# Weight low parts on one engine, modulation work spread anew: a two-layer hybrid backbone on one core

## The chip, the core and the metric

The kernel runs on one core of a Trainium2 chip. Its time is the device time of one execution in microseconds, the median of the runs shown. The engines are named as in the profile: TensorE (PE, its weight loads PEld), VectorE (DVE), ScalarE (ACT), GpSimd (POOL) and SyncE (SP), whose queue issues the weights' transfers.

## The reference

256 latent tokens and 256 context tokens of 1024 channels pass two layers. A layer is a SwiGLU half-step, four parallel token mixers with a gated merge, and a second half-step; each of the three has a norm that is shifted and scaled by vectors (modulation), which come from the conditioning vectors `c` and `c_ctx` by a large matrix product. Cut to what matters:

```python
def adaln(cvec, w, b):
    m = jax.nn.silu(cvec) @ w + b            # nine vectors of 1024 per layer
...
def ffn_half_step(s, g, mods, j, w1, w3, w2):
    h = modulate(rmsnorm(s, g), mods[j], mods[j + 1])
    return s + 0.5 * mods[j + 2] * swiglu(h, w1, w3, w2)
...
for i in range(DEPTH):
    x = ffn_half_step(x, ..., m_lat, 0, ...);  ctx = ffn_half_step(ctx, ..., m_ctx, 0, ...)
    # mixers: bidirectional gated linear attention (a scan), spatial gating, 2-D DFT, short convolution
    y = merge(h, branches, w_branch[i], w_gate[i], b_gate[i], w_out[i])
    x = x + m_lat[5] * y
    x = ffn_half_step(x, ..., m_lat, 6, ...)
    # the context gets the same in layer 0; in layer 1 it is only read by the scan
return rmsnorm(x, g_final)
```

The mixers are added up as `sigmoid(h @ w_gate[k] + b_gate[k]) * (branch[k] @ w_branch[k])` over the four branches, and the sum goes through `w_out`.

## The kernel before

Activations lie with channels on the partitions and the 512 tokens (latent 0 to 255, context 256 to 511) along the free axis. Every weight tile (128x1024) is used in a split form: `hi` is the tile cast to float32r by ScalarE (L79), `lo` is what the cast lost, `raw - hi` (L82); every activation has `hh` and `hl` in the same way. A product is three passes of matmuls (`passes`, L321): hi x hh, hi x hl, lo x hh.

The six stages are called here FFN 1 (layer 0, first half-step), mixer 1, FFN 2, FFN 3 (layer 1, first half-step), mixer 2 and FFN 4. FFN 4 and most of mixer 2 have the latent tokens alone, 256 columns; the others have both, 512.

The program is a list of units that `_Program` walks through in order; a unit has weight tiles and a function that issues the matmuls. Two rings of four buffers hold raw and split tiles. When a unit has used a tile it calls `release`, and `ahead` splits the next one, so four tiles are split in advance, in program order. Each engine has one queue and takes its instructions in that order. A tile whose entry has the mark "pool" gets its low part on GpSimd, others on VectorE. The marks come from tables (`DPOOL`, `HPOOL`, `DPOOL1`, `TPOOL`, `CPOOL`): every second up tile (w3), most w2 tiles where both streams run, two or four tiles of a head, some tiles of the merge and the convolution. `hold_lows` keeps low parts back from the end of a stage's tail until the next head calls `flush`.

A half-step has three parts (`PARTS`: 8, 8 and 6 tiles of the hidden axis). Each part has up steps (w1 and w3, `glu` makes the instructions g, L547, cast and gl, L335) and eight down steps (w2). In the third part the last three w2 tiles are the tail (`tail_group`): latent columns first, then context; after each product come the residual on VectorE (`residual`, L531), a square on ScalarE and its sum on GpSimd (`add_sq`, L366). The next stage's norm begins in the tail: `Norm.ms` sums the squares over channels by a matmul (L393), takes the power on GpSimd, `diag` (L402) makes a diagonal `dg` of it, `bc` (L406) spreads it by a matmul, and `scaled`, `high` and `low` make hn, hh and hl. `head_group` is the first unit of a stage; it starts with four tiles on the latent half (`pair_hi`, L450, where both streams run).

The modulation vectors are computed on VectorE by 128 modulation units (`ada_unit`, L290), each a 128x1024 tile of the modulation matrix with one instruction per conditioning vector (multiply, and sum along the free axis). 96 units have two (`junk` and `ada_raw`), the last 32 have one. `PHASES` says how many units `weave` puts behind a step of each kind, and `phase_end` how many must be through at the end of a stage: 32, 48, 80, 112, 120, 128.

In a mixer the scan (`gla_stream`) runs as a side program: after every so many columns of matmuls `tick` lets it go on to its next `yield`. Its seven levels end in score matmuls (lv, L709). Then come products K and Q (L717 to L721), transposes kt (L739), updates u (L748), and two blocks of outputs o (L781), each followed by square, sum, power and scaling into W (L784 to L789). `proj_r` drains what is left of the scan and, 24 matmuls later, transposes W (oT, L1118).

Of the kernel before, what the change touches and what calls it, by code (L numbers as in the profile page):

```python
# [7 lines left out]
F32 = mybir.dt.float32  # L8
# [36 lines left out]
class _Program:  # L45
# [28 lines left out]

    def split(self, raw, n, eng=None):
        nc, pool = self.nc, self.pool
        hi = pool.tile([128, 1024], F32R, tag="whi", name="whi", bufs=RING)
        lo = pool.tile([128, 1024], F32R, tag="wlo", name="wlo", bufs=RING)
        nc.scalar.copy(hi[:, :n], raw[:, :n])  # L79

        def low():
            (eng or nc.vector).tensor_tensor(lo[:, :n], raw[:, :n], hi[:, :n].bitcast(F32), ALU.subtract)  # L82

        if self.hold_lows:
            self.lows.append(low)
        else:
            low()
        return hi, lo
# [43 lines left out]
    def ahead(self, need=-1):  # L132
        while True:
            self.fetch_ahead(need)
            if self.ns >= len(self.todo):
                return
            f = self.todo[self.ns]
            uj, spec = self.flat[f]
            if self.raws[f] is None or self.held >= (self.limit if uj > need else RING):
                return  # L140
            self.held += 1
            self.fetched["w"] -= 1
            t = self.split(*self.raws[f], eng=self.nc.gpsimd if len(spec) > 2 else None)
            self.got.setdefault(uj, []).append(t)
            self.ns += 1
# [31 lines left out]
def kernel(ctx: ExitStack, tc: tile.TileContext, I, out: bass.AP):  # L177
# [203 lines left out]
    class Norm:  # L381
# [17 lines left out]
        def diag(self):  # L399
            ms = self.r  # L400
            dg = self.dg = tmp("dg")[:, 0:256].rearrange("p (u i) -> p u i", u=2)
            V.tensor_tensor(dg, ident.unsqueeze(1).to_broadcast([128, 2, 128]),  # L402
                            ms[:, 2:4].unsqueeze(2).to_broadcast([128, 2, 128]), ALU.mult)

# [27 lines left out]
        def low(self, c):  # L432
            l, m, st = self.l, self.m, c[0] // 256
            a, b = c[0], c[0] + c[1]
            for d in range(KT):
                t, hh = self.t[c][d], st8["hh"][:, d, a:b].bitcast(F32)
                if d % 2:
                    S.activation(out=t, in_=t, func=AF.Identity, bias=mod(l, m, d, st), scale=1.0)
                    G.tensor_tensor(st8["hl"][:, d, a:b], t, hh, ALU.subtract)  # L439
                else:  # L440
                    V.scalar_tensor_tensor(st8["hl"][:, d, a:b], t, mod(l, m, d, st), hh, ALU.add, ALU.subtract)

# [11 lines left out]
    def head_group(ws, accs, streams, done, skip=()):  # L454
# [42 lines left out]
    def tail_group(ds_, ws, rhs, nk, streams, gate, after, nxt):  # L497
# [21 lines left out]
        if CTX not in streams:  # L519
# [15 lines left out]
    def add_ffn(l, s, m, streams, after, weave, nxt):  # L535
# [63 lines left out]
        for pi, (f0, nf) in enumerate(PARTS):  # L599
            fs = list(range(f0, f0 + nf))  # L600
            if pi == 0:
                hw = [w(n, f) for f in (0, 1) for n in ("w1", "w3")]
                hw = [h + ("pool",) * (i in HPOOL[0 if l + s == 0 else len(streams)]) for i, h in enumerate(hw)]
                P.add(hw, head)
# [4 lines left out]
            for f in fs:  # L609
                P.add([w("w1", f), w("w3", f) + ("pool",)], up(f))  # L610
                if l == 0 and s == 0 and f == 2:
# [6 lines left out]
            def w2c(d):  # L618
                pl = ("pool",) if (d >= DPOOL if len(streams) == 2 else d in DPOOL1) else ()
                return ("w", I["w2"][l, s, d][:, f0 * 128:(f0 + nf) * 128]) + pl  # L620

# [12 lines left out]
    def gla_stream(l, c, A, want_o):  # L634
# [84 lines left out]
        if want_o:  # L719
            V.tensor_tensor(Q[lo_], Wr[lo_, :, tok], X[lo_], ALU.mult)  # L720
            V.tensor_tensor(Q[hi_], Wl[hi_, :, tok], Y[hi_], ALU.mult)  # L721
        yield

# [75 lines left out]
    def add_mixer(l, both, after, weave, nxt):  # L799
# [38 lines left out]

        P.add([wT(h) + ("pool",) * (h in HPOOL[2]) for h in range(4)], head)

# [255 lines left out]
        def add_terms(k, first=False, last=False, each=lambda dp: None):  # L1096
            for dp in range(4):
                pl = [("pool",) if i in TPOOL[l][k] else () for i in range(3)]
                P.add([("w", I["wgate"][l, k, 2 * dp]) + pl[0], ("w", I["wgate"][l, k, 2 * dp + 1]) + pl[1],
                       ("w", I["wbranch"][l, k, dp]) + pl[2]], term(k, dp, first, last))  # L1100
                each(dp)

        add_terms(1, first=True)
        for t_ in range(4):
            ws = [wT(i + t_) + (("pool",) if n in CPOOL[l] else ()) for n, i in enumerate((20, 24, 16))]
            P.add(ws, proj_conv(t_))
        add_terms(2)
# [25 lines left out]
        for h in range(4):  # L1133
            P.add([wT(4 + h)], proj_r(h))
            if h == 0:
                P.add([], load_cond)
# [48 lines left out]
    PHASES = [  # L1185
        (32, dict(head=0, up0=0.5, up=0.2, down0=1.25, down1=1.5, down2=1.2)),
        (48, dict(r=1, term0=3, term1=4, term2=3, term3=0, wout=1)),
        (80, dict(head=0, up0=0.5, up=0.2, down0=1.25, down1=1.5, down2=1.2)),
        (112, dict(head=0, up0=0.5, up=0.2, down0=1.25, down1=1.5, down2=1.2)),
        (120, dict(r=1, term0=1.5, term1=1.5, term2=1.5, term3=1.5, wout=0)),  # L1190
        (128, dict(head=2, up0=1, up=0, down0=0, down1=0, down2=0)),
    ]
# [177 lines left out]
```

## Time and profile before

| | |
|---|---|
| median of 3 runs | 2275.84 us (2275.73 to 2279.39) |
| profiled execution, its own time | 2279.79 us |
| span of the profiled execution | 2277.8 us |
| TensorE busy | 2214.9 us |
| VectorE busy | 1364.2 us, 1857 instructions |
| ScalarE busy | 769.9 us |
| GpSimd busy | 743.9 us, 437 instructions |
| transfers | 330.43 MB, 145 GB/s over the span |

Busy times overlap. Time in a stage is lost where TensorE stops, and the stages stop for different reasons, so the shares of the whole span say little: one has to find the stops in TensorE's timeline, and look at what the engine that is waited for was doing just before. The granted clock of TensorE is 1.00 (2.4 GHz) in most windows of 20 us and lower in those that contain a stop and the restart behind it.

### The profile page before, as it was taken

To read this page: it belongs to the slowest core of one execution; us is meant where nothing else is said; L and a number is where in the kernel's file an instruction comes from. 1 tells how busy PE (TensorE), PEld (TensorE's weight loads), DVE (VectorE), ACT (ScalarE), POOL (GpSimd) and SP (SyncE) were. 2 spreads that over 40 slices of the span, in tenths; PEclk is the share of its full clock that TensorE was granted. 3 is DMA by queue.
4 is the path that set the end of the run, shared out by engine and by line. 5 is a ranking of instruction groups with operands and counts; after the bars stand their busy time and mean duration, and the time that the engine had idled before them with its cause. 6 is when DMAs were issued, how large, how long until landed. Compare 5 with 4: busy or idle time off the path is not lost.

```text
span 2277.8 us, 31627 instructions
## 1 busy us (share of the span) xinstructions
PE 2214.9 (97%) x12718; PEld 1950.2 (86%) x12718; DVE 1364.2 (60%) x1857; ACT 769.9 (34%) x1090; POOL 743.9 (33%) x437
## 2 busy tenths in 40 slices
PE   6999999899999999999999999999999998998998
PEld 4888888898888888798888888888889998998998
DVE  4474575566657736853837464654435788875644
ACT  3322222443232223243232233222234553345443
POOL 1232425322213314142323263323334245424222
PEclk9999999999999999999999999999999999999999
DMA  7454454422222234523535433443544453485663
GB/s 271 158 164 150 132 180 140 128 82 69 89 84 84 84 111 153 208 99 123 176 129 167 137 112 122 154 151 120 185 148 146 137 166 106 142 278 191 223 187 115
DMA packets 98563, 330.43 MB, mean 145 GB/s; under 512 B 11505, under 2 KB 17649, under 8 KB 98161
## 3 DMA queue, kind: packets, MB, share of 16 engines
q1 hardware_dynamic: 90480, 315.91, 42.5%
q10 hardware_dynamic: 7936, 12.50, 1.5%
q8 instruction: 100, 1.64, 0.3%
q14 instruction: 47, 0.38, 0.0%
HBM read 322.08 MB, written 6.29 MB: 144 GB/s over the span
## 4 chain that ended last, share of the span: by engine, by line
PE 84%; DVE 8%; issue 2%; DMA 2%; ACT 2%; POOL 2%; POOLq 0%; DVEq 0%; ACTq 0%; SPq 0%
PE mm L321 74%; PE mm L867 4%; PE dn L321 1%; DVE ada_raw L290 1%; PE lv L709 1%; DVE junk L290 1%; DVE wlo L82 1%; DMA ada_raw<-in_wadaT_dram 1%; ACT whi L79 1%; POOL wlo L82 1%; DMA x<-in_xT_dram 1%; ACT hh L429 1%; DMA raw<-in_w_dram 1%; PE mm L450 1%; PE ms L393 0%
## 5 line engine op out<-in xcount | busy, mean ns | idle before, releaser
L321 PE MATMUL mm<-hh,whi 128*128 128x512 f32 (+1 forms) x2448 | 843.8, 349 | 3.3 <-ACT hh L429 2.3
L321 PE MATMUL mm<-hh,wlo 128*128 128x512 f32 (+1 forms) x2448 | 837.8, 346 | 6.3 <-DVE wlo L82 4.1
L321 PE MATMUL mm<-hl,whi 128*128 128x512 f32 (+1 forms) x2512 | 808.9, 343 | 0.1
L82 POOL TENSOR_TENSOR wlo<-raw,whi 128x1024 fp32r<-128x1024 f32 (+1 forms) x183 | 472.0, 2582 | 900.7 <-ACT whi L79 872.6
L79 ACT CAST whi<-raw 128x1024 fp32r<-128x1024 f32 (+2 forms) x458 | 469.0, 1032 | 751.5 <-PE mm L321 412.9
L82 DVE TENSOR_TENSOR wlo<-raw,whi 128x1024 fp32r<-128x1024 f32 (+3 forms) x275 | 349.4, 1276 | 352.9 <-ACT whi L79 349.4
L321 PEld LDWEIGHTS mm<-hh,wlo 128*128 128x128 f32 x2448 | 468.5, 191 | 62.8 <-DVE wlo L82 5.1
L321 PEld LDWEIGHTS mm<-hh,whi 128*128 128x128 f32 x2448 | 469.0, 192 | 59.3 <-ACT hh L429 3.2
L321 PEld LDWEIGHTS mm<-hl,whi 128*128 128x128 f32 x2512 | 454.2, 190 | 54.3 <-POOL hl L439 0.3
L290 DVE SCALAR_TENSOR_TENSOR ada_raw<-ada_raw,condb 128x1024 f32<-128x1024 f32 x128 | 250.1, 1956 | 18.0 <-DMA ada_raw<-in_wadaT_dram 14.7
L321 PE MATMUL mm<-gh,whi 128*128 128x512 f32 (+1 forms) x710 | 248.6, 350 | 0.0
L321 PE MATMUL mm<-gl,whi 128*128 128x512 f32 (+1 forms) x710 | 247.7, 349 | 0.0
L321 PE MATMUL mm<-gh,wlo 128*128 128x512 f32 (+1 forms) x710 | 247.5, 349 | 0.0
L547 DVE TENSOR_TENSOR g<-sg,mm 128x512 f32<-128x512 f32 (+1 forms) x88 | 54.5, 620 | 247.5 <-PE mm L321 243.0
L334 ACT CAST gh<-g 128x512 fp32r<-128x512 f32 (+1 forms) x88 | 49.9, 567 | 352.0 <-DVE g L547 352.0
L290 DVE SCALAR_TENSOR_TENSOR junk<-ada_raw,condb 128x1024 f32<-128x1024 f32 x96 | 147.3, 1535 | 10.5 <-DMA ada_raw<-in_wadaT_dram 10.3
L321 PEld LDWEIGHTS mm<-gh,whi 128*128 128x128 f32 x710 | 136.1, 192 | 16.9
L321 PEld LDWEIGHTS mm<-gl,whi 128*128 128x128 f32 x710 | 136.0, 192 | 16.9
L321 PEld LDWEIGHTS mm<-gh,wlo 128*128 128x128 f32 x710 | 136.0, 191 | 16.5
L531 DVE SCALAR_TENSOR_TENSOR x<-mm,mods,x 128x256 f32<-128x256 f32 x180 | 78.5, 476 | 28.7 <-PE mm L321 28.5
L335 DVE TENSOR_TENSOR gl<-g,gh 128x512 fp32r<-128x512 f32 (+1 forms) x88 | 58.8, 668 | 55.7 <-ACT gh L334 55.7
L366 POOL TENSOR_TENSOR sq<-sq,sqt 128x256 f32<-128x256 f32 (+1 forms) x44 | 50.2, 1140 | 104.5 <-ACT sqt L365 103.5
(222 smaller groups left out, 2360.3 us busy)
## 6 DMA issues: line engine op xcount, KB each, us to landing
raw<-in_w_dram SPq DMA_DIRECT2D x240, 512.0 KB, 3.6
ada_raw<-in_wadaT_dram SPq DMA_DIRECT2D x128, 512.0 KB, 4.4
raw<-in_wgate_dram SPq DMA_DIRECT2D x64, 512.0 KB, 3.7
raw<-in_winT_dram SPq DMA_DIRECT2D x56, 512.0 KB, 3.4
raw<-in_wbranch_dram SPq DMA_DIRECT2D x32, 512.0 KB, 3.6
raw<-in_w_dram SPq DMA_DIRECT2D x32, 384.0 KB, 3.1
ada_raw<-in_wada_dram SPq DMA_DIRECT2D x16, 512.0 KB, 6.2
raw<-in_wout_dram SPq DMA_DIRECT2D x16, 512.0 KB, 5.8
```

Of the source, the lines that this page charges most:

```text
L79: nc.scalar.copy(hi[:, :n], raw[:, :n])
L82: (eng or nc.vector).tensor_tensor(lo[:, :n], raw[:, :n], hi[:, :n].bitcast(F32), ALU.subtract)
L290: V.scalar_tensor_tensor(o, raw, 1.0, ada["c"][st], ALU.mult, ALU.mult, accum_out=mods[l][:, 8 * m + d, st:st + 1])
L321: T.matmul(acc[:, c0:c0 + cw], lhsT=a, rhs=b[:, c0:c0 + cw], start=bool(first and i == 0), stop=bool(last and i == n - 1))
L334: S.copy(dst_hi[:, a:b], src[:, a:b])
L335: V.tensor_tensor(dst_lo[:, a:b], src[:, a:b], dst_hi[:, a:b].bitcast(F32), ALU.subtract)
L366: eng.tensor_tensor(sq[:, a:b], sq[:, a:b], t[:, a:b], ALU.add)
L429: S.activation(out=st8["hh"][:, d, a:b], in_=self.t[c][d], func=AF.Identity, bias=mod(l, m, d, st), scale=1.0)
L450: T.matmul(acc[:, sl], lhsT=w3(w[part])[:, k, :], rhs=hsrc(k)[0][:, sl], start=(k == 0 and part == 0), stop=False)
L531: V.scalar_tensor_tensor(x[:, d, a:b], acc[:, a:b], gate(d, s[0] // 256), x[:, d, a:b], ALU.mult, ALU.add)
L547: V.tensor_tensor(g[:, a:b], sg[:, a:b], p3[:, a:b], ALU.mult)
L867: T.matmul(p[:, 0:width], lhsT=x_, rhs=w_[:, u, :], start=(k + i == 0), stop=(k == KT - 1 and i == 2))
```

## The change

All low parts of weight tiles go to VectorE, and the tables that marked tiles for GpSimd are gone. The odd halves of `hl`, which ScalarE and GpSimd made, are made on VectorE like the even ones. `diag` has two instructions with a scalar operand in place of one with two tensors. Low parts are also held from the single-stream tail (end of mixer 2) to the head of FFN 4. In the scan one `yield` becomes `yield 2`: the piece behind it, the transposes kt, comes two ticks later instead of one. The modulation units are all done by the end of FFN 3, by 40, 48, 88 and 128 at the end of the first four stages, with none in the third part's down steps and none in mixer 2 and FFN 4; so the conditioning vectors are not loaded again in mixer 2.

```diff
-DPOOL = 1
-HPOOL = ((), (0, 1, 2, 3), (0, 1))
...
-DPOOL1 = ()
-TPOOL = (((0, 1, 2), (), (), ()), ((0,), (0,), (0,), ()))
-CPOOL = ((), (0,))
...
         def low():
-            (eng or nc.vector).tensor_tensor(lo[:, :n], raw[:, :n], hi[:, :n].bitcast(F32), ALU.subtract)
+            nc.vector.tensor_tensor(lo[:, :n], raw[:, :n], hi[:, :n].bitcast(F32), ALU.subtract)
...
-            V.tensor_tensor(dg, ident.unsqueeze(1).to_broadcast([128, 2, 128]),
-                            ms[:, 2:4].unsqueeze(2).to_broadcast([128, 2, 128]), ALU.mult)
+            for u in range(2):
+                V.tensor_scalar(dg[:, u, :], ident, ms[:, 2 + u:3 + u], None, ALU.mult)
...
-                if d % 2:
-                    S.activation(out=t, in_=t, func=AF.Identity, bias=mod(l, m, d, st), scale=1.0)
-                    G.tensor_tensor(st8["hl"][:, d, a:b], t, hh, ALU.subtract)
-                else:
-                    V.scalar_tensor_tensor(st8["hl"][:, d, a:b], t, mod(l, m, d, st), hh, ALU.add, ALU.subtract)
+                V.scalar_tensor_tensor(st8["hl"][:, d, a:b], t, mod(l, m, d, st), hh, ALU.add, ALU.subtract)
...
                 if CTX not in streams:
+                    P.hold_lows = False
+                    P.flush()
                     N.low(LAT)
...
             N.diag()
             for _ in ds_:
                 P.release()
+                P.hold_lows = True
...
-                P.add([w("w1", f), w("w3", f) + ("pool",)], up(f))
+                P.add([w("w1", f), w("w3", f)], up(f))
...
             V.tensor_tensor(Q[hi_], Wl[hi_, :, tok], Y[hi_], ALU.mult)
-        yield
+        yield 2
...
-            if h == 0:
+            if h == 0 and both:
                 P.add([], load_cond)
...
     PHASES = [
-        (32, dict(head=0, up0=0.5, up=0.2, down0=1.25, down1=1.5, down2=1.2)),
-        (48, dict(r=1, term0=3, term1=4, term2=3, term3=0, wout=1)),
-        (80, dict(head=0, up0=0.5, up=0.2, down0=1.25, down1=1.5, down2=1.2)),
-        (112, dict(head=0, up0=0.5, up=0.2, down0=1.25, down1=1.5, down2=1.2)),
-        (120, dict(r=1, term0=1.5, term1=1.5, term2=1.5, term3=1.5, wout=0)),
-        (128, dict(head=2, up0=1, up=0, down0=0, down1=0, down2=0)),
+        (40, dict(head=0, up0=1, up=1.15, down0=1, down1=1.25, down2=0)),
+        (48, dict(r=1, term0=3, term1=3, term2=0, term3=0, wout=0)),
+        (88, dict(head=0, up0=0.8, up=1.15, down0=1, down1=1.5, down2=0)),
+        (128, dict(head=0, up0=0.8, up=1.15, down0=1, down1=1.5, down2=0)),
     ]
```

Every other place where a tile had the mark "pool" loses it in the same way. In the orders below the changed kernel has its own line numbers (L77 is the low part, L285 the modulation unit, L525 the residual).

VectorE at the end of FFN 1, in part 3's down steps, before (x is the residual, mods the sum that ends a group of eight units):

```order
L290 SCALAR_TENSOR_TENSOR junk,mods_87<-ada_raw,condb 128x1024
L290 SCALAR_TENSOR_TENSOR ada_raw,mods_87<-ada_raw,condb 128x1024
L531 SCALAR_TENSOR_TENSOR x<-mm,mods_87,x 128x256 x4
...
L531 SCALAR_TENSOR_TENSOR x<-mm,mods_87,x 128x256 x2
...
L294 TENSOR_TENSOR mods_87<-mods_87,bada 128x16
L531 SCALAR_TENSOR_TENSOR x<-mm,mods_87,x 128x256 x5
L396 TENSOR_SCALAR ms<-ms 128x2
```

The same place in the change:

```order
L77 TENSOR_TENSOR wlo<-raw,whi 128x768 x2
L525 SCALAR_TENSOR_TENSOR x<-mm,mods_87,x 128x256 x4
L77 TENSOR_TENSOR wlo<-raw,whi 128x768
L525 SCALAR_TENSOR_TENSOR x<-mm,mods_87,x 128x256 x2
L77 TENSOR_TENSOR wlo<-raw,whi 128x768
L525 SCALAR_TENSOR_TENSOR x<-mm,mods_87,x 128x256 x2
L77 TENSOR_TENSOR wlo<-raw,whi 128x1024
L525 SCALAR_TENSOR_TENSOR x<-mm,mods_87,x 128x256 x5
L391 TENSOR_SCALAR ms<-ms 128x2
```

Between two steps' residuals stood a unit of two instructions; there is now one low part.

VectorE at the end of the scan in mixer 2, from the scaling of the first block of outputs to the first `proj_r` (W is the scaled output, sig a term of the merge, rs the product that takes the transposed W), before:

```order
L789 TENSOR_TENSOR W<-o,oms 128x4x128
L82 TENSOR_TENSOR wlo<-raw,whi 128x1024
L1080 TENSOR_TENSOR sig<-sig,mm 128x256
L82 TENSOR_TENSOR wlo<-raw,whi 128x1024
L786 TENSOR_REDUCE oms<-Y 128x4
L787 TENSOR_SCALAR oms<-oms 128x4
L789 TENSOR_TENSOR W<-o,oms 128x4x128
L82 TENSOR_TENSOR wlo<-raw,whi 128x1024
L1080 TENSOR_TENSOR sig<-sig,mm 128x256
...
L1121 SCALAR_TENSOR_TENSOR rs<-mm,ggla,rs 128x256
```

The same place in the change:

```order
L781 TENSOR_TENSOR W<-o,oms 128x4x128
L77 TENSOR_TENSOR wlo<-raw,whi 128x1024
L1072 TENSOR_TENSOR sig<-sig,mm 128x256
L778 TENSOR_REDUCE oms<-Y 128x4
L779 TENSOR_SCALAR oms<-oms 128x4
L781 TENSOR_TENSOR W<-o,oms 128x4x128
L77 TENSOR_TENSOR wlo<-raw,whi 128x1024
L1111 SCALAR_TENSOR_TENSOR rs<-mm,ggla,rs 128x256
```

The second block's sum came after one more tile, and the last two terms of the merge behind it; it now comes right behind the first block's, and `proj_r` right behind that. On TensorE 36 matmuls stood between the two blocks of outputs and 60 between the second and oT; now none and 24.

## Rows read from the trace of the kernel before

**Rows 1.** The page's first part: busy time of each engine.
```profile
PE 2214.9 (97%) x12718; PEld 1950.2 (86%) x12718; DVE 1364.2 (60%) x1857; ACT 769.9 (34%) x1090; POOL 743.9 (33%) x437
```
**Rows 2.** Chain that ended last, mixer 1: start us, us, what.
```profile
734.02 12.26 PE mm L321 x54
```
**Rows 3.** Timeline of FFN 1: start us, us, engine, line, operation, out<-in, idle before.
```profile
88.01 0.69 DVE L335 TENSOR_TENSOR gl<-g,gh 128x512 fp32r<-128x512 f32 x1 [0.69 <-ACT gh L334]
88.61 1.22 DVE L290 SCALAR_TENSOR_TENSOR junk<-ada_raw,condb 128x1024 f32<-128x1024 f32 x1
89.01 3.08 POOL L82 TENSOR_TENSOR wlo<-raw,whi 128x1024 fp32r<-128x1024 f32 x1 [8.49 <-ACT whi L79]
...
89.88 3.29 DVE L290 SCALAR_TENSOR_TENSOR ada_raw<-ada_raw,condb 128x1024 f32<-128x1024 f32 x1
```
**Rows 4.** Groups by form: busy us, mean ns | idle before.
```profile
L82 POOL TENSOR_TENSOR wlo<-raw,whi 128x1024 fp32r<-128x1024 f32 x162 | 425.0, 2625 | 849.1 <-ACT whi L79 821.1 <-issue 13.8 <-DMA bgate<-in_bgate_dram 7.7
L82 DVE TENSOR_TENSOR wlo<-raw,whi 128x1024 fp32r<-128x1024 f32 x258 | 332.2, 1293 | 323.0 <-ACT whi L79 319.5 <-PE sgu L946 2.3 <-PE mm L321 0.5
...
L290 DVE SCALAR_TENSOR_TENSOR ada_raw<-ada_raw,condb 128x1024 f32<-128x1024 f32 x128 | 250.1, 1956 | 18.0 <-DMA ada_raw<-in_wadaT_dram 14.7
...
L290 DVE SCALAR_TENSOR_TENSOR junk<-ada_raw,condb 128x1024 f32<-128x1024 f32 x96 | 147.3, 1535 | 10.5 <-DMA ada_raw<-in_wadaT_dram 10.3
```
**Rows 5.** Groups by form: the residual.
```profile
L531 DVE SCALAR_TENSOR_TENSOR x<-mm,mods,x 128x256 f32<-128x256 f32 x180 | 78.5, 476 | 28.7 <-PE mm L321 28.5
```
**Rows 6.** Timeline of TensorE, tails of FFN 1, 2 and 3.
```profile
389.64 0.28 PE L321 MATMUL mm<-gh,whi 128*128 128x256 f32 x1
...
403.44 1.87 PE L393 MATMUL ms<-ones,sq 128*128 128x1 f32 x8 [5.00 <-POOL sq L366]
...
411.42 0.40 PE L450 MATMUL mm<-hh,whi 128*128 128x256 f32 x2
...
1338.89 0.28 PE L321 MATMUL mm<-gh,whi 128*128 128x256 f32 x1
...
1359.62 0.40 PE L450 MATMUL mm<-hh,whi 128*128 128x256 f32 x2
...
1709.91 0.28 PE L321 MATMUL mm<-gh,whi 128*128 128x256 f32 x1
...
1724.17 0.40 PE L450 MATMUL mm<-hh,whi 128*128 128x256 f32 x2
```
**Rows 7.** Windows, end of mixer 1: PE, PEld, DVE, ACT, POOL busy, PEclk, DMA share, GB/s.
```profile
940.00:960.00 20.00, 16.34 (x63) 12.42 (x62) 15.50 (x22) 6.60 (x8) 1.54 (x1) 0.91 0.68 263
```
**Rows 8.** Windows from one block of score matmuls to the next, mixer 2.
```profile
1886.69:1901.69 15.00, 12.26 (x90) 12.06 (x90) 13.42 (x15) 4.49 (x7) 8.29 (x5) 0.89 0.39 128
1901.69:1914.83 13.14, 11.28 (x91) 10.56 (x89) 11.84 (x15) 5.28 (x8) 6.03 (x4) 1.00 0.39 127
1914.83:1927.30 12.47, 10.90 (x88) 10.52 (x89) 9.80 (x12) 3.87 (x6) 8.48 (x6) 1.00 0.40 129
...
1939.70:1950.54 10.84, 10.66 (x88) 10.48 (x89) 10.51 (x13) 3.90 (x5) 7.04 (x5) 1.00 0.48 147
```
**Rows 9.** Timeline of TensorE, the two blocks of transposes kt in mixer 2.
```profile
1841.85 1.06 PE L739 MATMUL kt<-ident,K 128*128 128x128 f32 x8 [1.38 <-DVE K L718]
...
1971.21 1.49 PE L739 MATMUL kt<-ident,K 128*128 128x128 f32 x8 [3.51 <-DVE K L718]
```
**Rows 10.** Timeline of TensorE and VectorE: the second block of outputs in mixer 2.
```profile
1991.72 0.39 PE L782 MATMUL o<-S,Q 128*128 128x128 f32 x2
...
1994.80 0.69 DVE L789 TENSOR_TENSOR W<-o,oms 128x512 f32<-128x512 f32 x1 [1.13 <-POOL oms L788]
```
**Rows 11.** Timeline of the head of FFN 4.
```profile
2069.26 2.56 DVE L402 TENSOR_TENSOR dg<-ident,ms 128x256 f32<-128x256 f32 x1 [0.82 <-POOL ms L397]
...
2071.88 0.79 PE L406 MATMUL ms<-dg,ones 128*128 128x256 f32 x1 [3.64 <-DVE dg L402]
```
**Rows 12.** Timeline of TensorE, first steps of FFN 4.
```profile
2108.63 0.39 PE L321 MATMUL mm<-hh,wlo 128*128 128x256 f32 x1 [0.76 <-POOL wlo L82]
```

More of the change, by code (lines that the diff above doesn't have):

```diff
@@ L73, in fetch, with split @@
         return raw, n
-    def split(self, raw, n, eng=None):
+    def split(self, raw, n):
         nc, pool = self.nc, self.pool
@@ L137, in ahead @@
             f = self.todo[self.ns]
-            uj, spec = self.flat[f]
+            uj = self.flat[f][0]
             if self.raws[f] is None or self.held >= (self.limit if uj > need else RING):
@@ L142, in ahead @@
             self.fetched["w"] -= 1
-            t = self.split(*self.raws[f], eng=self.nc.gpsimd if len(spec) > 2 else None)
+            t = self.split(*self.raws[f])
             self.got.setdefault(uj, []).append(t)
@@ L602, in add_ffn @@
                 hw = [w(n, f) for f in (0, 1) for n in ("w1", "w3")]
-                hw = [h + ("pool",) * (i in HPOOL[0 if l + s == 0 else len(streams)]) for i, h in enumerate(hw)]
                 P.add(hw, head)
@@ L618, in w2c @@
             def w2c(d):
-                pl = ("pool",) if (d >= DPOOL if len(streams) == 2 else d in DPOOL1) else ()
-                return ("w", I["w2"][l, s, d][:, f0 * 128:(f0 + nf) * 128]) + pl
+                return ("w", I["w2"][l, s, d][:, f0 * 128:(f0 + nf) * 128])
             nd = KT - 3 if lastp else KT
@@ L837, in head @@
             head_group(ws, accs, streams, done, skip)
-        P.add([wT(h) + ("pool",) * (h in HPOOL[2]) for h in range(4)], head)
+        P.add([wT(h) for h in range(4)], head)
         def load_small():
@@ L1097, in add_terms @@
             for dp in range(4):
-                pl = [("pool",) if i in TPOOL[l][k] else () for i in range(3)]
-                P.add([("w", I["wgate"][l, k, 2 * dp]) + pl[0], ("w", I["wgate"][l, k, 2 * dp + 1]) + pl[1],
-                       ("w", I["wbranch"][l, k, dp]) + pl[2]], term(k, dp, first, last))
+                P.add([("w", I["wgate"][l, k, 2 * dp]), ("w", I["wgate"][l, k, 2 * dp + 1]),
+                       ("w", I["wbranch"][l, k, dp])], term(k, dp, first, last))
                 each(dp)
@@ L1104, in add_mixer @@
         for t_ in range(4):
-            ws = [wT(i + t_) + (("pool",) if n in CPOOL[l] else ()) for n, i in enumerate((20, 24, 16))]
-            P.add(ws, proj_conv(t_))
+            P.add([wT(i + t_) for i in (20, 24, 16)], proj_conv(t_))
         add_terms(2)
```

## Prediction, made before the change was run

> **What bounds the kernel now.** I read the page first, then the windows of 20 us, then TensorE's own timeline for the places where it waits, and last the queues that it waits for. The page has TensorE at work for 97% of the span [rows 1]: where it runs free it issues a 512-column matmul every 12.26/54 = 0.227 us [rows 2], and no edit here changes that. So only its stops can be won, and they lie in few places: the ends of the first two SwiGLU half-steps (FFN 1, FFN 2), the end of mixer 1, nearly all of the second half of mixer 2, and the head of the last half-step (FFN 4).
>
> The cause of most of them shows in VectorE's and GpSimd's rows. The modulation instruction that VectorE began at 88.61, ahead of GpSimd, took 1.22 us; the next, of the same size, was issued at 89.88, while GpSimd computed a low part from 89.01 to 92.09, took 3.29 us and ended at 93.17, as if it had begun to run when GpSimd was through [rows 3]. The means carry this: 1.96 and 1.54 us for the modulation instructions, 1.29 for VectorE's own low parts, 2.63 for GpSimd's [rows 4]. A low part on GpSimd thus stopped a busy VectorE for 3.29 - 1.22 = 2.07 us, longer than the 1.29 us that VectorE needs for one.
>
> **The change part by part.** Times are summed against the profiled execution, 2279.79 us (its span is 2277.8), which stands 3.95 us above the median of 2275.84.
>
> Lows in the half-steps, at nothing. By the listed order 183 lows leave GpSimd. A step of part 2's down projection gives TensorE 24 x 0.227 = 5.45 us. At its highest rate, 1.5 units a step (FFN 2), VectorE gets 1.5 x 2 x 1.27 us (from one start to the next [rows 3]) + one low of 1.29 + two residuals of 0.48 [rows 4, 5] = 6.06 us. That is 0.6 us over, 5 us after eight steps. The cover is the ring: four tiles are split ahead, so a low has three tiles, 16 us, to arrive, and part 3's up steps then give VectorE time again: a pair of tiles gives TensorE 10.9 us and VectorE 2 lows, g and gl of 0.69 each [rows 3] and 1.15 units, 6.9 us. FFN 1 at 1.25 units needs 5.4 us. FFN 3 has one instruction per unit for all but its first eight units. If the cover fails, each late step costs its 0.6 us; both ends are 0 and +5, and I take 0. The later issue of unit transfers on the SP queue and the weights behind them is covered by the same 16 us.
>
> Tails of FFN 1 and FFN 2: -7.5 and -6.5 us. From the first 256-column matmul of the tail to the first of the next head TensorE takes 411.42 - 389.64 = 21.78 us in FFN 1, 1359.62 - 1338.89 = 20.73 in FFN 2, and 1724.17 - 1709.91 = 14.26 in FFN 3 [rows 6], with the same matmuls in between. FFN 3 has one instruction per unit and is through with them earlier; in the others units stand between the residuals on VectorE and lows between the sums of squares on GpSimd, as the order shows, the squares come late, and in FFN 1 TensorE waits 5.00 us for them [rows 6] and restarts at the lower clock. The change has no unit in part 3's down steps and no low on GpSimd, so both should take FFN 3's 14.26. Bounds: 0, if the residuals are late for another reason, and -14.
>
> End of mixer 1: -5. The window 940 to 960 has TensorE busy for 16.34 us at a granted clock of 0.91 [rows 7]: 3.7 us idle and up to 1.8 lost at 1.2 GHz. The waits are for a low and the last merged tiles, behind ten units in the last branch's four terms. Six units now stand in the first two of them, none in the last two or in wout. Bounds 0 and -5.5.
>
> Mixer 2: -10.6. This sum has four terms.
> (1) The scan's levels. TensorE works in cycles of 72 matmuls and one block of score matmuls. Four cycles in which GpSimd also has a low took 15.00, 13.14 and 12.47 us and about the last again; the cycle after them, whose lows are all on VectorE already, took 10.84 [rows 8]. That is the best evidence that the move pays where VectorE is nearly full: one low more on VectorE, and the cycle is shorter. The two convolution cycles have more VectorE work, and I let them go to 11.3; the terms go to 10.9. Gain 3.7 + 1.8 + 1.6 + 1.6 = 8.7. Bounds: 0 and -11.
> (2) The doubled yield gives VectorE two ticks in place of one (36 matmuls each) for its products ahead of the transposes, which now wait 1.38 and 3.51 us [rows 9]; with about 1 us at the lower clock behind the longer one, -5.9.
> (3) It also shifts the rest of the scan by two ticks, and that is paid at the end. The second block of outputs lost the 36 matmuls ahead of it and follows on the first; between it and the transposes oT stand 24 matmuls, 2.9 us, where there were 60. The chain behind the outputs (square, sum, power on GpSimd, scaling) took from 1992.11, the last output's end, to 1995.49 [rows 10], 3.4 us for one block, and two must now pass through it with a low between them: about 6 us after the last output. TensorE waits 3 us at oT and restarts at the lower clock for another 1: +4. Bounds 0 and +6.
> (4) Units gone from its terms: 0, as TensorE ran free there.
> Here a page speaks against the change. The row says that a low costs TensorE less on a VectorE at 13.42 of 15.00 us than on GpSimd [rows 8]. The Trainium skill, Perfetto Trace Analysis, Optimizing Scalar/DVE Operations, says that offloading from a saturated DVE to ScalarE or even GpSimd may make sense, and in the next sentence that between DVE and GpSimd it might not help. By its first half the cycles would win nothing, 0 in place of -8.7, and the second rival's time follow; the cycle of 10.84 us bears out the second half.
>
> Head of FFN 4: -2.9. The diagonal dg takes 2.56 us behind the first of GpSimd's lows, and TensorE waits 3.64 for it [rows 11]; an instruction of its width takes 0.48 [rows 5], so -2.1. With the lows and units gone a wait of 0.76 us for a GpSimd low [rows 12] goes too. Bounds 0 and -4. The new hold keeps two lows behind the norm, where their tiles are not used until those of two others are through.
>
> The other norms: -1. The hl parts move to VectorE, 44 of them at some 0.48 us (the residual's, of the same width [rows 5]), half of it given back as GpSimd no longer reads beside it; two narrow dg instructions for one wide one, each shown by no row: between -0.5 and +0.4 us at each of four heads. I take -0.25.
>
> Sum: -7.5 - 6.5 - 5 - 8.7 - 5.9 + 4 - 2.9 - 1 = -33.5 us. 2279.8 - 33.5 = 2246.3 as a profiled execution, and less 3.95 a median of **2242 us**.
>
> **Rivals.**
> *Everything fits.* The chain at oT hides and all cycles go to 10.84: 4 + 1 + 2 us more, 2235. For it: the terms' cycles are already that short. Against it: two blocks back to back.
> *VectorE stays the bound of mixer 2.* Its 18 lows, 23 us, go to an engine that is busy for 13.42 of 15.00 us [rows 8], and the cycles stay as they are: 8.7 us of the gain is lost, some of the transposes' too: 2254. It is what the Trainium skill's first half would have. Against it: the 10.84.
> *Lows late behind units.* VectorE is one queue: a unit whose transfer is late now stops the lows behind it, which GpSimd's queue let pass. The cover of 16 us is gone when transfers and units add up to that, and then the half-steps give back the tails: about 20 us, 2262.
> *Slower.* The modulation instructions are long of themselves or for the DMA's writes, and not for GpSimd's lows. Then they stay at 1.96 and 1.54, lows at 1.29 [rows 4]. A down step in FFN 2 needs 1.5 x 3.66 + 1.29 + 0.95 = 7.7 us against 5.45, +18 us in eight steps; one in FFN 1 6.8, +11; mixer 2 gets 18 x 1.29 = +23. Together +52, against 25 that the tails and the heads still bring: 2303. It decides from 5.45 us of VectorE work a step. Against it: 3.29 us that ends just after GpSimd's low [rows 3].
> That the units are not gone from the tails is excluded: the listed order shows them gone.
>
> **How the numbers follow.** A measurement can tell about 0.2%, 4.6 us, from no change. Chances: my sum 0.58, everything fits 0.14, VectorE bound 0.16, lows late 0.07, slower 0.05. All but the last are faster by over 0.2%; for mixtures of late lows with a weaker mixer I leave 0.03 to no change. So faster 0.91, same 0.03, slower 0.06. My sum's own bounds are 2234 to 2250; 8 in 10 reaches to the first two rivals, 2232 to 2257.
>
> **What would show it.** Modulation instructions at a mean of 1.25 to 1.35 us, VectorE's lows at 1.25, VectorE busy for about 1440 us, GpSimd for about 240. Both tails at 14 to 15 us. Cycles in mixer 2 near 11 us, transposes kt without a wait, a wait of 2 to 4 us at the first oT. dg under 0.6 us in FFN 4's head. I am wrong if TensorE waits for lows inside the half-steps, if modulation instructions stay near 1.9 us, or if the cycles stay at 12 to 15 us.

## The result, and the profile after

The change runs in 2253.27 us (median of 4 runs, 2252.54 to 2253.84), the kernel before on the same chip in 2275.78: a ratio of 0.9898, interval 0.988 to 0.9915. That is 22.5 us less, where 33.5 was forecast: faster, 11.3 us above the forecast of 2242, within the range but outside the bounds of my own sum, 2234 to 2250. The profiled executions are 26.0 us apart (2253.79 against 2279.79).

The page's first part: the work left GpSimd, and VectorE's busy time rose by 62 us only [rows 1].

```profile
PE 2209.4 (98%) x12718; PEld 1946.2 (86%) x12718; DVE 1425.7 (63%) x2096; ACT 753.7 (33%) x1046; POOL 230.8 (10%) x210
```

Groups by form on VectorE (busy us, mean ns | idle before). Low parts of 1024 columns went from 258 to 420 instructions, and the modulation instructions from 1956 and 1535 ns [rows 4] to what one takes alone [rows 3]:

```profile
L77 DVE TENSOR_TENSOR wlo<-raw,whi 128x1024 fp32r<-128x1024 f32 x420 | 522.5, 1251 | 333.2 <-ACT whi L74 328.9 <-PE sgu L938 2.3 <-DMA wconv<-in_wconv_dram 0.3
L285 DVE SCALAR_TENSOR_TENSOR ada_raw<-ada_raw,condb 128x1024 f32<-128x1024 f32 x128 | 156.1, 1223 | 7.3 <-DMA ada_raw<-in_wadaT_dram 3.9
L285 DVE SCALAR_TENSOR_TENSOR junk<-ada_raw,condb 128x1024 f32<-128x1024 f32 x96 | 116.9, 1217 | 2.9 <-DMA ada_raw<-in_wadaT_dram 2.9
```

To see where the 26.0 us came from, the span is cut at one recurring event: the sums of squares with which TensorE begins the last norm ahead of each stage. TensorE's timeline of the kernel before has them here (start us, us):

```profile
42.41 1.25 PE L393 MATMUL ms<-ones,sq 128*128 128x1 f32 x8 [1.55 <-DVE sq L375]
...
415.26 0.95 PE L393 MATMUL ms<-ones,sq 128*128 128x1 f32 x8
...
992.13 0.95 PE L393 MATMUL ms<-ones,sq 128*128 128x1 f32 x8
...
1363.46 0.95 PE L393 MATMUL ms<-ones,sq 128*128 128x1 f32 x8
...
1728.01 0.95 PE L393 MATMUL ms<-ones,sq 128*128 128x1 f32 x8
2066.23 0.28 PE L393 MATMUL ms<-ones,sq 128*128 128x1 f32 x2
...
2266.91 0.36 PE L393 MATMUL ms<-ones,sq 128*128 128x1 f32 x2
```

and that of the change here:

```profile
41.75 1.71 PE L388 MATMUL ms<-ones,sq 128*128 128x1 f32 x8 [1.82 <-DVE sq L370]
...
408.87 0.95 PE L388 MATMUL ms<-ones,sq 128*128 128x1 f32 x8
...
979.33 0.95 PE L388 MATMUL ms<-ones,sq 128*128 128x1 f32 x8
...
1343.83 0.95 PE L388 MATMUL ms<-ones,sq 128*128 128x1 f32 x8
...
1708.71 0.95 PE L388 MATMUL ms<-ones,sq 128*128 128x1 f32 x8
2042.38 0.28 PE L388 MATMUL ms<-ones,sq 128*128 128x1 f32 x2
...
2240.22 0.35 PE L388 MATMUL ms<-ones,sq 128*128 128x1 f32 x2
```

Differences of neighbours give the stages (the stretches ahead of the first and behind the last cancel to 0.03 us; the forecast has a quarter of a us for each norm in it):

| stage | before | change | difference | forecast |
|---|---|---|---|---|
| FFN 1 | 372.85 | 367.12 | -5.7 | -7.8 |
| mixer 1 | 576.87 | 570.46 | -6.4 | -5.3 |
| FFN 2 | 371.33 | 364.50 | -6.8 | -6.8 |
| FFN 3 | 364.55 | 364.88 | +0.3 | -0.3 |
| mixer 2 | 338.22 | 333.67 | **-4.6** | **-10.6** |
| FFN 4 | 200.68 | 197.84 | -2.8 | -2.9 |

Mixer 2 is far off, and FFN 1 falls 2.1 us short; the rest comes within 1.1 us. In the tails the two distances that [rows 6] show as 21.78 and 20.73 us are now 14.42 and 14.32:

```profile
390.52 0.28 PE L316 MATMUL mm<-gh,whi 128*128 128x256 f32 x1
...
404.94 0.50 PE L441 MATMUL mm<-hh,whi 128*128 128x256 f32 x2
...
1325.63 0.28 PE L316 MATMUL mm<-gh,whi 128*128 128x256 f32 x1
...
1339.95 0.45 PE L441 MATMUL mm<-hh,whi 128*128 128x256 f32 x2
```

The window that answers to [rows 7], as far ahead of its norm, has TensorE at work throughout:

```profile
927.00:947.00 20.00, 20.00 (x90) 16.57 (x89) 9.30 (x13) 6.63 (x8) 1.29 (x1) 1.00 0.35 116
```

Mixer 2's level cycles, as windows from one block of score matmuls to the next (the first three and the last of six; us, PE, PEld, DVE, ACT, POOL busy, PEclk). VectorE is busy for 95% of the third and of the last, the second became longer than it was [rows 8], and the fourth and fifth, not shown, took 10.93 and 11.38 us:

```profile
1868.34:1879.74 11.40, 10.69 (x91) 10.46 (x89) 9.97 (x13) 4.49 (x7) 4.88 (x3) 1.00 0.45 138
1879.74:1894.13 14.39, 11.11 (x90) 10.59 (x89) 11.27 (x14) 9.04 (x12) 4.48 (x4) 1.00 0.36 110
1894.13:1906.21 12.08, 12.08 (x88) 12.08 (x89) 11.52 (x14) 2.84 (x4) 6.07 (x5) 0.86 0.41 132
...
1928.52:1939.88 11.36, 10.92 (x89) 10.54 (x89) 10.81 (x13) 3.90 (x6) 6.08 (x5) 1.00 0.43 140
```

Behind the levels the two waits at kt [rows 9] are gone, a low part behind the second now stops TensorE instead, and oT waits (the window 1970 to 1980 has a granted clock of 0.83):

```profile
1824.71 1.04 PE L731 MATMUL kt<-ident,K 128*128 128x128 f32 x8
...
1950.96 1.03 PE L731 MATMUL kt<-ident,K 128*128 128x128 f32 x8
...
1953.95 0.39 PE L316 MATMUL mm<-hh,wlo 128*128 128x256 f32 x1 [1.72 <-DVE wlo L77]
...
1973.85 0.48 PE L1108 MATMUL oT<-ident,W 128*128 128x128 f32 x1 [2.83 <-DVE W L781]
```

### The profile page after: what moved, and what is told of

Read it like the earlier page. It is cut to its first block, busy times and chain, and to the rows that moved or that the text cites. A ratio compares the mean times of both kernels' runs of the same rounds, so it can differ in the third digit from the quotient of the medians.

```text
span 2251.8 us, 31437 instructions
## 1 busy us (share of the span) xinstructions
PE 2209.4 (98%) x12718; PEld 1946.2 (86%) x12718; DVE 1425.7 (63%) x2096; ACT 753.7 (33%) x1046; POOL 230.8 (10%) x210
## 5 line engine op out<-in xcount | busy, mean ns | idle before, releaser
L77 DVE TENSOR_TENSOR wlo<-raw,whi 128x1024 fp32r<-128x1024 f32 (+2 forms) x458 | 560.5, 1230 | 366.1 <-ACT whi L74 361.4
L285 DVE SCALAR_TENSOR_TENSOR ada_raw<-ada_raw,condb 128x1024 f32<-128x1024 f32 x128 | 156.1, 1223 | 7.3 <-DMA ada_raw<-in_wadaT_dram 3.9
L361 POOL TENSOR_TENSOR sq<-sq,sqt 128x256 f32<-128x256 f32 (+1 forms) x44 | 41.4, 941 | 1077.3 <-issue 856.2
L285 DVE SCALAR_TENSOR_TENSOR junk<-ada_raw,condb 128x1024 f32<-128x1024 f32 x96 | 116.9, 1217 | 2.9 <-DMA ada_raw<-in_wadaT_dram 2.9
L525 DVE SCALAR_TENSOR_TENSOR x<-mm,mods,x 128x256 f32<-128x256 f32 x180 | 78.4, 476 | 19.2 <-PE mm L316 19.2
L859 PE MATMUL mm<-whi,hh 128*128 128x256 f32 (+1 forms) x224 | 64.4, 288 | 0.0
```

What stands on the lines that cost most here:

```text
L77: nc.vector.tensor_tensor(lo[:, :n], raw[:, :n], hi[:, :n].bitcast(F32), ALU.subtract)
L285: V.scalar_tensor_tensor(o, raw, 1.0, ada["c"][st], ALU.mult, ALU.mult, accum_out=mods[l][:, 8 * m + d, st:st + 1])
L361: eng.tensor_tensor(sq[:, a:b], sq[:, a:b], t[:, a:b], ALU.add)
L525: V.scalar_tensor_tensor(x[:, d, a:b], acc[:, a:b], gate(d, s[0] // 256), x[:, d, a:b], ALU.mult, ALU.add)
L859: T.matmul(p[:, 0:width], lhsT=x_, rhs=w_[:, u, :], start=(k + i == 0), stop=(k == KT - 1 and i == 2))
```

## The experiments

The theory after the result: GpSimd's reads did stop VectorE, and moving the low parts was right everywhere; what mixer 2 lacks is taken by (a) GpSimd's remaining products K (L682, L683) and sums m (L1085), which still stop VectorE, and (b) the doubled yield, which costs more than it saves. Rivals: VectorE is simply full there, or modulation instructions got shorter for their new places and not for GpSimd. "Mixer 2" below is the stage time of the table. Ratios are against the kernel before on the same chip.

| kernel | us | ratio | mixer 2 |
|---|---|---|---|
| the change | 2253.27 | 0.9898 | 333.67 |
| before, units spread anew | 2259.96 | 0.9918 | 338.23 |
| change, units as before | 2260.23 | 0.9920 | 333.66 |
| change, memsets on GpSimd | 2278.97 | 1.0002 | 355.10 |
| change, mixer 2's lows back | 2257.59 | 0.9907 | 338.94 |
| change, K on VectorE | 2247.63 | 0.9870 | 329.26 |
| change, K and m on VectorE | 2249.65 | 0.9873 | 329.30 |
| change, single yield | 2249.90 | 0.9880 | 329.75 |
| change, double yield in the latent stream alone | 2246.91 | 0.9865 | 327.67 |
| K and m on VectorE, single yield | 2247.62 | 0.9863 | 328.27 |
| the same, 1.5 yields in the latent stream | 2244.42 | 0.9858 | 325.50 |

Intervals of the ratios reach 0.0009 to 0.0018 to either side, so neighbours in time are told apart by their stage times in mixer 2, which agree to 0.02 us where code and order are the same there (338.22 and 338.23). Each is from one profiled execution, and other stages agree less well: with the same code FFN 1 takes 365.59 us in one run and 367.12 in another, FFN 4 197.15 and 198.44. A us or two of a whole time is therefore not decided here.

**The two halves of the change.** First the new spread of units alone, in the kernel before:

```diff
     PHASES = [
-        (32, dict(head=0, up0=0.5, up=0.2, down0=1.25, down1=1.5, down2=1.2)),
...
+        (40, dict(head=0, up0=1, up=1.15, down0=1, down1=1.25, down2=0)),
...
-            if h == 0:
+            if h == 0 and both:
                 P.add([], load_cond)
```

> The kernel before with only the units spread as in the change; low parts on GpSimd as before, dg and hl as before, single yield. Theory: modulation instructions stay at 1.6 to 2.0 us as GpSimd still computes 183 lows; the tails get most of their gain (15 to 18 us), the end of mixer 1 its 5, the cycles of mixer 2 stay at 12 to 15 us, dg in FFN 4's head as before: 2260 to 2266. Rival, modulation instructions are long by what stands around them in the old spread: they fall to 1.3 us here too, and the time to 2254 or less.

Then its opposite, the change with the old table of phases:

```diff
     PHASES = [
-        (40, dict(head=0, up0=1, up=1.15, down0=1, down1=1.25, down2=0)),
...
+        (32, dict(head=0, up0=0.5, up=0.2, down0=1.25, down1=1.5, down2=1.2)),
...
-            if h == 0 and both:
+            if h == 0:
```

> The change, with the units where they were before (old table of phases, two tiles of conditions loaded in mixer 2 again); all low parts on VectorE. Theory: modulation instructions stay at 1.22 us without a low on GpSimd; the tails of FFN 1 and FFN 2 give back part, as 1.2 to 1.5 units stand between two residuals again (2.4 to 3.7 us of VectorE), 16 to 19 us in place of 14.4; the end of mixer 1 gives back 2 to 5 us, mixer 2 some 3 for 8 units in full cycles: 2260 to 2267. Rival, the low parts were all of it: tails 14 to 15 us, 2252 to 2256.

Groups by form, the kernel before with units spread anew:

```profile
L290 DVE SCALAR_TENSOR_TENSOR ada_raw<-ada_raw,condb 128x1024 f32<-128x1024 f32 x128 | 282.3, 2208 | 15.2 <-DMA ada_raw<-in_wadaT_dram 11.8
L290 DVE SCALAR_TENSOR_TENSOR junk<-ada_raw,condb 128x1024 f32<-128x1024 f32 x96 | 140.6, 1465 | 12.7 <-DMA ada_raw<-in_wadaT_dram 11.4 <-ACT condb L281 1.2
```

With low parts on GpSimd the modulation instructions stay long on the whole wherever they stand; with low parts on VectorE and units in the old places they are short (means of 1299 and 1217 ns). The rival falls. The tails: with new units alone 14.26 and 14.25 us, below the 15 to 18 that I expected, so the units account for all of the gain there, and low parts between GpSimd's squares for none. With the old units and low parts on VectorE 18.40 and 16.52: short units cost 4.0 and 2.2 us where long ones cost 7.4 and 6.4. The squares are late there as in [rows 6], by half as much (TensorE's timeline of that run):

```profile
398.46 1.32 PE L388 MATMUL ms<-ones,sq 128*128 128x1 f32 x8 [2.36 <-POOL sq L361]
```

Mixer 2 does not feel the units at all: 338.23 against 338.22 in the kernel before, 333.66 against 333.67 in the change, where I had expected some 3 us.

By stages, either half alone brings most of what the two bring in the first three. In FFN 1, mixer 1 and FFN 2 the new units alone take 7.5, 6.2 and 6.5 us off, with modulation instructions as slow as before; the rest of the change alone takes 4.9, 4.9 and 4.6; both take 5.7 (with a lower clock at the start of FFN 1, see below), 6.4 and 6.8. Summed over the six stages it is 20.8, 21.1 and 26.0 us. Only mixer 2 and most of the head of FFN 4 need the rest of the change.

**Reading or working?** GpSimd gets a memset of each low tile ahead of VectorE's low part, so it writes for 401 us in all (its low parts of 1024 columns took 425 before [rows 4]) and reads no more than in the change:

```diff
         def low():
+            if n == 1024:
+                nc.gpsimd.memset(lo[:, :n].bitcast(F32), 0.0)
             nc.vector.tensor_tensor(lo[:, :n], raw[:, :n], hi[:, :n].bitcast(F32), ALU.subtract)
```

> The change, with a memset of the low tile on GpSimd ahead of each of VectorE's 1024-column low parts (same tile, GpSimd busy some 0.96 us for each, writing only). Theory, a GpSimd operation that reads two operands is what stops VectorE, and one that only writes does not: modulation instructions stay at 1.22 to 1.3 us, low parts at 1.23 to 1.3, within 4 us of the change. Rival, any work of GpSimd stops it: modulation instructions at 1.6 us or more.

Its timeline has a memset in the middle of a modulation instruction, which takes 1.23 us as ever; the means stay at 1224 and 1218 ns:

```profile
255.26 1.23 DVE L287 SCALAR_TENSOR_TENSOR ada_raw<-ada_raw,condb 128x1024 f32<-128x1024 f32 x1
255.86 0.95 POOL L78 MEMSET wlo<- 128x1024 f32 x1 [4.49 <-PE mm L318]
```

So it is not any work of GpSimd that stops VectorE; a low part differs from a memset by its two reads and its length. The Trainium skill, SBUF — State Buffer, Who interferes with whom, says the same: a VectorE instruction with two inputs from SBUF contends with a GpSimd instruction that reads SBUF, not with one that only writes. The forecast of the time failed: 25.7 us more than the change, 21.4 of them in mixer 2. A low part now also waits for its memset, which shares GpSimd's one queue with K and m (by the groups, VectorE stood idle for 260 us in all ahead of low parts that waited for memsets). An engine that stops no other can still be late.

**GpSimd's remaining reads in mixer 2.** First low parts back on GpSimd there:

```diff
+TPOOL = (((), (), (), ()), ((0,), (0,), (0,), ()))
+CPOOL = ((), (0,))
...
-            nc.vector.tensor_tensor(lo[:, :n], raw[:, :n], hi[:, :n].bitcast(F32), ALU.subtract)
+            (eng or nc.vector).tensor_tensor(lo[:, :n], raw[:, :n], hi[:, :n].bitcast(F32), ALU.subtract)
```

> The change, but the 13 low parts of mixer 2 that before were GpSimd's (the first tile of each convolution step and of each step of three terms) are GpSimd's again. My theory, a low part costs TensorE more on GpSimd than on a nearly full VectorE: the cycles of the scan go back to 12.4 to 13 us, 6 to 9 us more than the change, 2259 to 2262. The rival, VectorE is the bound there and the move won nothing: the cycles stay at 11 to 12 us or get shorter, 2250 to 2254.

It is 16 low parts, not 13: four steps of convolution and twelve of terms, and GpSimd's instructions go from 210 to 226. Mixer 2 takes 5.3 us more, less than I expected, but against the rival; the intervals of the two ratios overlap, so the whole time does not tell. The cycles are 12.99, 13.18, 14.31, 10.87, 11.03 and 11.37 us: the last three stay as short as in the change, against my theory, and the six together take 73.8 us for 71.5. The other 3.1 us lie ahead of the levels (1.6) and behind them (1.4). The Trainium skill, Perfetto Trace Analysis, Optimizing Scalar/DVE Operations, lets one offload from a saturated VectorE and doubts it between VectorE and GpSimd; the doubt holds here, by these 5.3 us. Then the opposite, K on VectorE as well:

```diff
-                G.tensor_tensor(Kb[lo_, :, :, 0], Wlb[lo_, :, :, 0], Yb[lo_, :, :, 0], ALU.mult)
-                G.tensor_tensor(Kb[hi_, :, :, 1], Wrb[hi_, :, :, 1], Xb[hi_, :, :, 1], ALU.mult)
+                V.tensor_tensor(Kb[lo_, :, :, 0], Wlb[lo_, :, :, 0], Yb[lo_, :, :, 0], ALU.mult)
+                V.tensor_tensor(Kb[hi_, :, :, 1], Wrb[hi_, :, :, 1], Xb[hi_, :, :, 1], ALU.mult)
...
-        G.tensor_tensor(K[lo_], Wl[lo_, :, tok], Y[lo_], ALU.mult)
+        V.tensor_tensor(K[lo_], Wl[lo_, :, tok], Y[lo_], ALU.mult)
```

> The change, with the scan's key products K moved from GpSimd to VectorE as well (three lines, both mixers). Theory, it is GpSimd's remaining products that hold VectorE in mixer 2: beside them the query products Q take 1.75 and 1.66 us and two low parts 4.68; alone a product should take about 0.69 (the row of X, twice its partitions), four of them 2.8 us in place of 3.4, and the stall of 2.5 us at 1879.74 goes: 4 to 6 us less than the change, 2247 to 2249. Rival, VectorE is full by its own work: two products more a cycle of 0.7 to 1.2 us each, over seven cycles 10 to 17 us more, 2263 to 2270.

and m too, in mixer 2 (`both` is false there):

```diff
-                        G.tensor_tensor(m[d][:, a:b], m[d][:, a:b], sg[u][:, a:b], ALU.add)
+                        (G if both else V).tensor_tensor(m[d][:, a:b], m[d][:, a:b], sg[u][:, a:b], ALU.add)
```

> As the run with K on VectorE, and the sums m of mixer 2's terms on VectorE too (0.41 us each). Theory: what is moved costs 0.82 us a cycle and frees 0.44 us of two low parts and some of the copies; so within 2 us of the run with K alone, 2246 to 2250, with low pairs at 2.45 in place of 2.89 us. Rival, VectorE full: another 0.8 us in each of eight term steps, 6 us above the run with K alone.

The change's timeline of one level's products, K on GpSimd and Q on VectorE:

```profile
1902.01 1.28 POOL L682 TENSOR_TENSOR K<-W,Y 64x512 f32<-64x512 f32 x1
1902.09 1.75 DVE L680 TENSOR_TENSOR Q<-W,X 64x512 f32<-64x512 f32 x1 [0.47 <-POOL Q L679]
...
1903.37 1.61 POOL L683 TENSOR_TENSOR K<-W,X 64x512 f32<-64x512 f32 x1
...
1903.87 1.66 DVE L681 TENSOR_TENSOR Q<-W,Y 64x512 f32<-64x512 f32 x1
```

The same level with K on VectorE, four products in 2.8 us where two took 3.4:

```profile
1902.94 0.68 DVE L680 TENSOR_TENSOR Q<-W,X 64x512 f32<-64x512 f32 x1 [0.46 <-POOL Q L679]
1903.64 0.69 DVE L681 TENSOR_TENSOR Q<-W,Y 64x512 f32<-64x512 f32 x1
1904.34 0.68 DVE L682 TENSOR_TENSOR K<-W,Y 64x512 f32<-64x512 f32 x1
1905.04 0.69 DVE L683 TENSOR_TENSOR K<-W,X 64x512 f32<-64x512 f32 x1
```

VectorE does more and is done sooner. The six cycles fall from 71.5 us in sum to 68.2, with m to 67.4, and the last two with m to 10.51 and 10.50, where TensorE is busy for all of it. Mixer 2 gains 4.4 us; m gives 0.7 us in the cycles and loses it again behind them (oT waits 3.24 us for 2.85), so that the two runs are equal. The forecast for the stop in the second cycle fell in part: TensorE's stop near its head, 1.43 us for the convolution's y on VectorE, stays in both with its length unchanged, so it is not K's doing (the one at its end, at the next score matmuls, goes from 1.85 us to 1.14 and 1.02). Nothing was tried on it.

**The yield.** The double yield undone:

```diff
             V.tensor_tensor(Q[hi_], Wl[hi_, :, tok], Y[hi_], ALU.mult)
-        yield 2
+        yield
```

> The change, with the double yield before the transposes kt undone. My sum: the two waits at kt come back (1.4 and 3.5 us and 1 us at the lower clock, +5.9) and the wait at oT goes (-4), net +1.9, 2255. Rival a, the low part behind kt was the real wait and moves with it: no kt wait above 1 us, oT gone, -3, 2250. Rival b, the wait at oT stays since the chain behind the outputs is late for VectorE's sake: +5.9, 2259.

and, the scan running twice (context, st = 1, then latent), undone in the first alone:

```diff
-        yield 2
+        yield 1 if st else 2
```

> The change, with the double yield only in the latent stream (the second pair of transposes kt and the outputs), single in the context stream. From the traces of the change and of the run with the single yield, the double yield saves 3.1 us at kt and costs 2.0 for a low part behind kt, 4.6 at oT and 1.5 in the level cycles. Theory, kt and oT belong to the latent stream's yield, the cycles (and the place of the first kt) to the context stream's: from the norm ahead of mixer 2 to FFN 4's 329.75 + 3.5 = 333.3 us, the cycles sum to 69.9 as with the single yield, oT waits 3.05. Rival, the cycles are long for the latent stream's yield or by chance of the order: they sum to 71.5, and the time is above the change's 333.67.

TensorE's timeline, single yield: the first pair of transposes waits no more than with the double one, the second as before:

```profile
1819.43 0.82 PE L731 MATMUL kt<-ident,K 128*128 128x128 f32 x6
...
1944.02 1.06 PE L731 MATMUL kt<-ident,K 128*128 128x128 f32 x8 [3.49 <-DVE K L710]
```

Double in the latent stream alone: no wait at either, and next to none at oT:

```profile
1820.29 1.03 PE L731 MATMUL kt<-ident,K 128*128 128x128 f32 x8
...
1945.57 1.04 PE L731 MATMUL kt<-ident,K 128*128 128x128 f32 x8
...
1969.25 0.33 PE L1108 MATMUL oT<-ident,W 128*128 128x128 f32 x1 [0.46 <-DVE W L781]
```

The first time was that of rival a, but not for its reason: kt still waits 3.49 us, where it had none above 1. The second was below theory and rival. Together they give the price of each delay. Mixer 2 is 338.23 us with lows on GpSimd, 329.75 with the rest of the change and a single yield (-8.5), 327.67 with the latent stream's double yield (-2.1), 333.67 with the context's too (+6.0). The context's removes no wait, as the first pair of transposes had lost its own to the faster VectorE; it only moves 36 matmuls (4.3 us) from behind the levels to ahead of them. Against the run without it the cycles take 71.5 us for 70.0, and the stretch from the last level's scores to FFN 4's norm 102.5 for 101.2, although 4.3 us of its work are gone: 5.6 us more are lost there (the low behind kt, 1.72 us, the wait at oT, 2.83 for 0.46, and the lower clock behind it), less 1.2 us saved ahead of the levels. Why the cycles become longer is not shown, and the context's double yield was not run alone. My forecast that oT would wait as long with the latent yield alone was wrong: with this one alone the chain has room.

**Both together.** K and m on VectorE with the single yield, and then with one and a half in the latent stream:

> K and m on VectorE and the single yield together, on top of the change. In the traces K on VectorE took 4.4 us off mixer 2 and its head behind (333.7 to 329.3 us from the norm ahead of mixer 2 to that of FFN 4), the single yield 3.9. Theory, they are separate (cycles by contention; oT and the alignment by the yield): about 8 us less than the change, 2244 to 2246, cycles at 10.5 to 10.9, no wait at oT, the wait at kt 2 us or less as its K now takes 1.22 us. Rival, both remove the same idle time: 2248 to 2250, as either alone.

```diff
-        yield 2
+        yield 1 if st else 1.5
```

> K and m on VectorE and the single yield in the context stream, as in the best run so far, but one and a half yields (54 matmuls) in the latent stream. Theory, kt then waits about 2 us less than its 3.8 and the 42 matmuls that stand between the second outputs and oT, 5.0 us, nearly hide the chain of 6 us there: 1 to 2 us less than the best run, 326.5 to 327.5 us from norm to norm. Rival, the wait at oT does not shrink in proportion since the chain of the two outputs meets low parts: 328 us or more.

The first came out between theory and rival in time, and its second kt still waits 3.78 us. In mixer 2 it takes 5.4 us off where K and m (4.4) and the single yield (3.9) alone sum to 8.3, so in part both remove the same idle time. The second has the lowest median here, 2244.42 us (ratio 0.9858, interval 0.9843 to 0.9872, which overlaps those of the next ones). Its mixer 2, 325.50 us, is 8 us below the change's and 1 below its forecast, with less than half the wait at kt and none at oT:

```profile
1943.16 1.06 PE L731 MATMUL kt<-ident,K 128*128 128x128 f32 x8 [1.65 <-DVE K L710]
...
1968.24 0.38 PE L1108 MATMUL oT<-ident,W 128*128 128x128 f32 x2
```

## Why the prediction was right, and where not

- **The cause** of the long instructions was right: GpSimd's low parts stopped VectorE, and without them the means fell a little below the forecast (1.22 us measured, 1.25 to 1.35 forecast; VectorE busy 1425.7 us for 1440, GpSimd 230.8 for 240). The runs with units and low parts exchanged and with memsets show it. But most of the time won does not hang on it: the new places of the units alone bring 20.8 of the 26.0 us. The prediction gave them a share in the tails and the end of mixer 1 and did not say that they could have nearly all of it there.
- **Lows in the half-steps at nothing:** right. FFN 3 moved by 0.3 us.
- **Tails -7.5 and -6.5:** measured -7.4 and -6.4. Of the two reasons that I gave, only the units between the residuals is shown; the low parts between the squares cost nothing. FFN 1 as a stage gained 5.7 us only, 1.7 less than its tail, since its first 6 us ran at the lower clock (1.2 GHz; granted 0.50 from 42 to 48 us). The window 40 to 60 had a granted clock of 0.91 before, 0.83 in the change, and 0.91 again in the run with the single yield, whose code is the same there and whose FFN 1 takes 1.5 us less. So the change of code is not the reason; what is was not tested.
- **End of mixer 1 -5:** -6.4 for the stage, and the new units alone bring 6.2 of it (570.71), the rest of the change alone 4.9.
- **Mixer 2 -10.6: measured -4.6, and this is the step that failed,** in terms (2) and (3). I gave the doubled yield -5.9 at kt and +4 at oT, -1.9 together. It measured +3.9 (329.75 to 333.67). The first of the two waits at kt was credited to it though the low parts removed it; the second was replaced in part by the low behind kt (1.72 us); and the chain at oT, sized rightly at 2.83 us of waiting, was not the whole price of two ticks. Low parts and all else bring -8.5, and that this is near term (1)'s -8.7 is chance: the six cycles give 4.8 of it (69.9 us for 74.7), and the rest lies ahead of them, the first wait at kt included, and behind them. With the single yield the four term cycles take 10.84 to 10.99 us, as forecast from the cycle of 10.84, while the two with convolution work take 12.93 and 13.41 for the 11.3 that I let them go to. For those I had no row and took the short cycle's side. In the change two of the six cycles (14.39 and 12.08 us) lie in the 12 to 15 us that I had named as a sign of being wrong.
- What I did not cost at all: GpSimd's K and m, which stay and stop VectorE more now that all low parts are there. Moving K is worth 4.4 us, m nothing more. The rows of Q in the trace of before would have shown it: 0.68 us in a cycle where no K runs beside it, 1.75 beside K.

```profile
1898.98 0.68 DVE L688 TENSOR_TENSOR Q<-W,X 64x512 f32<-64x512 f32 x1
...
1923.72 1.75 DVE L688 TENSOR_TENSOR Q<-W,X 64x512 f32<-64x512 f32 x1 [2.57 <-POOL Q L687]
```

- **Head of FFN 4 -2.9:** -2.8. TensorE waits 1.56 us for dg instead of 3.64, as the two narrow instructions take 0.48 us together. The form of dg and the low parts beside it changed at once, so which of them it was is not shown. The new units alone bring 1.0 of the 2.8.

```profile
2045.42 0.48 DVE L398 TENSOR_SCALAR dg<-ident,ms 128x128 f32<-128x128 f32 x2 [0.82 <-POOL ms L392]
```

- **From profile to median:** I took off 3.95 us, as the profiled execution before lay that much above its median. That of the change lies 0.5 above its own. Of the 11.3 us of error 7.5 are in the sum (2253.8 for 2246.3), 3.4 here, and the rest is rounding.
- The rivals: "VectorE stays the bound of mixer 2" gave 2254, the time that came. Its mechanism is not what happened: moving more work onto VectorE made mixer 2 shorter. That the time lay in the range is therefore not to my sum's credit: the range reached to this rival, and that its number came by another way was luck. The rival *slower* fell with the means of 1.22 us. So did *lows late behind units*: from 45 to 390, 1000 to 1325, 1350 to 1690 and 2055 to 2230 us TensorE has no stop above 0.3 us.

## What to carry to other kernels

Before an engine is called full, look at what runs beside it: an instruction of VectorE with two operands in SBUF that takes 1.75 us beside a reading GpSimd and 0.68 without is mostly waiting, and giving VectorE GpSimd's share can shorten its queue. And when a side program's step is delayed to hide one wait, check for each pass of it whether that wait is still there after the rest of the change; a delay that hides nothing is paid later: here a first one gained 2.1 us and a second on top of it lost 6.0. And when two changes touch one place, run each alone before the gain is put down to either.

## What the runs showed that I had not expected

- The contention depends on the kind of VectorE instruction. In the change a sum m on GpSimd took 1.58 us beside low parts (at 1897.34) and 0.74 us beside a masked copy from PSUM (at 1900.42), and the two copies then took 1.36 us, as without it. The Trainium skill, SBUF — State Buffer, Who interferes with whom, says that a VectorE instruction with at most one input from SBUF, outside its 2-port modes, does not contend with GpSimd; these rows agree.
- GpSimd's low parts became slower when the units moved alone, 2762 ns for 2625 [rows 4]: as if the stop worked both ways; no run tested that by itself.
- Two changes can share one gain: the units' new places bring 7.5 us in FFN 1's tail without any low part moved, and the low parts bring 3.4 of the same 7.4 with the units left in place.
